# Ten value tiles of an odd layer's projection moved into the seven-product pairs

## The chip, the cores and the metric

The kernel runs on one core of one Trainium2 chip. Its time is the device time of one execution in microseconds; a run's figure is compared by the median. The core has a matrix engine (PE, with a queue of weight loads PEld), a vector engine (DVE), an activation engine (ACT), a general engine (POOL), and a sync engine (SP) whose queue issues most DMAs. PE multiplies a 128 x 128 tile of weights that it has loaded with a moving tile of up to 512 columns and accumulates in PSUM. Each engine takes its instructions in one order, fixed when the program is compiled.

## The reference

One step of a two-layer trunk over 512 sample tokens and 128 prompt tokens, model width 2048, all in float32. Layer 0 has windowed attention (A) and a short gated convolution (B), layer 1 has differential attention (C) and dense attention with normed queries and keys (D). What matters here is layer 1:

```python
def odd_mixer(h, w_in, w_out, cqn, ckn, c_lam, c_on, dqn, dkn, lam_init, ctx=None, rope=None):
    cq, ck, cv, cg, dq, dk, dv, dg = split_cols(h @ w_in, ODD_SPLIT)
    ...
        cv_all = jnp.concatenate([ctx[1], cv], axis=2)
        dv_all = jnp.concatenate([ctx[3], v_d], axis=2)
    ...
    o1 = attend(cq[:, 0][:, :, None], ck_all[:, 0], cv_all)[:, :, 0]
    o2 = attend(cq[:, 1][:, :, None], ck_all[:, 1], cv_all)[:, :, 0]
    o_c = rms_norm(o1 - lam.astype(o1.dtype) * o2, c_on) * (1.0 - lam_init)
    y_c = o_c.transpose(0, 2, 1, 3).reshape(b, t, C_W) * jax.nn.silu(cg)
    y_d = merge_heads(attend(q_d, dk_all, dv_all)) * jax.nn.silu(dg)
    return jnp.concatenate([y_c, y_d], axis=-1) @ w_out, new
```

Each layer also makes a shift, a scale and a gate from `silu(cond) @ ada_w + ada_b` (the conditioning). The prompt tokens' new keys and values are outputs too. C has 4 heads, each with two maps of 128-wide queries and keys and one 256-wide value; D has 8 query heads and 2 heads of keys and values, 128 wide. So the projection of layer 1 has 8 + 8 + 8 + 8 tiles of 128 columns for cq, ck, cv, cg, and 8 + 2 + 2 + 8 for dq, dk, dv, dg: 52 tiles, ten of them values.

## The kernel before

All 640 tokens lie along the moving side as two halves of 320 (`HALF`). A projection tile is one block of 128 output columns; its sum runs over 16 row blocks of 128 (`KT`). Float32 accuracy comes from splitting both operands into a high and a low part (`split`, lines 240 to 242: ACT writes the high part, DVE the rest) and adding three products, high x high, high x low and low x high (lines 276 to 278). The weights of a tile come in four "quarters" of four row blocks, 256 KB each; SP reads them up to five quarters ahead (`RAW_AHEAD`) and they are split three ahead (`SPLIT_AHEAD`).

There are two ways to compute a tile. `run_tiles` (line 312) takes them singly. `run_pairs` (line 435) takes two tiles at once: weights and tokens are cut into 2 x 2 blocks, and seven products of sums of blocks stand for eight (a scheme of Winograd's and Strassen's kind, named Q1, Q2, N5, P6, P7, P4, Q3). DVE forms the sums of weight blocks and adds the results; the sums of the token blocks are formed once in advance (`forms`, tiles T0 to T7).

Layer 1 runs in these stages. `project` (line 1114) computes "front" tiles: 14 of the 16 gate tiles, first three as leading tiles while the rows h are made, then three singly, then eight in four pairs. A gate's result goes to the scratch `gdram` in DRAM (`gate_out`, `front_begin`, `front_done`). Then `run_tiles` computes 38 single tiles: q, k, v in the order of the attention, and last the two gates 4 and 5 (`very_late_gate`). Then `project_out(1, ...)` multiplies by the output weights: three leading tiles, during which the 16 row blocks of y are read back from `ydram` and split (`y1_maker`), three single tiles, and five pairs.

The work between the quarters is a set of generators. After each quarter `slot` (line 301) advances `prep` (a finished tile's own work, such as `k_gen` or `v_gen`), then `attn` (attention: one step each time the pace has summed up to 1), then the conditioning `fill` (`ada_on_dve`: a step reads 128 KB and makes two multiply-adds of 128 x 256 on DVE, line 213; each of its four blocks of 33 steps is tied to the weights split at its start). Attention takes 12 steps for a pair of D's heads (`pair_gen`) and 13 for a head of C (`diff_gen`), a step being roughly the scores and softmax of one block of 128 queries and the value products of the block before. In the stage of 38 tiles the attention takes one step a quarter, 1.5 in the last two tiles; the conditioning takes one step a quarter from the 17th quarter on. The order that a program states is a priority: the framework's planner may put later instructions first where an earlier one isn't ready, within the buffers that there are.

A value tile's `v_gen` copies the projection from PSUM to a buffer (`stage`), transposes it to rows (five transposes), splits it into `vh` and `vl` beside the cached values (`ctx_v`), writes the prompt's rows out, and starts the attention that needs it. Before a head's keys or values are overwritten, `drain(attn)` takes all steps that are left.

Of the kernel before, what the change touches and what calls it, by code (L numbers as in the profile page):

```python
# [48 lines left out]
FILL1 = 1.0  # L49
FILL1_FROM = 16  # L50
# [3 lines left out]
def trunk_kernel(ctx: ExitStack, tc: tile.TileContext, I: dict, O: dict):  # L54
# [523 lines left out]
    def k_gen(ap, pp, tag, src, gain, new_out):  # L578
        raw = ap.tile([P, 2, P], F32, tag="ctxk", name="ctxk", bufs=1)
        nc.sync.dma_start(raw, src.rearrange("(c p) d -> p c d", p=P))  # L580
        x = stage(ap, pp)
        yield
# [39 lines left out]
        split(hi[:, CTX + NS:CTX + NT], lo[:, CTX + NS:CTX + NT], t)  # L622

# [48 lines left out]
    def v_gen(ap, pp, src, new_out, w=P, j=0, then=None):  # L672
        x = stage(ap, pp)
        yield
        if j == 0:
            drain(attn)
            st["v"] = tuple(ap.tile([P, 7, w], F32R, tag=t, name=t) for t in ("vh", "vl"))
            ctx_v(ap, src, *st["v"], w)
        hi, lo = st["v"]
        cols = slice(j * P, (j + 1) * P)  # L680
        t = to_rows(cols_of(x), True)
        split(hi[:, 2:6, cols], lo[:, 2:6, cols], t.rearrange("p (b f) -> p b f", b=4))
# [3 lines left out]
        split(hi[:, 6, cols], lo[:, 6, cols], vp)  # L686
        nc.gpsimd.dma_start(new_out, vp)
        if then:
            attn.append(then())
# [141 lines left out]
    xdram, hdram, gdram = ([dram.tile([P, NT], F32, name=f"{n}{k}") for k in range(KT)] for n in ("xd", "hd", "gd"))  # L831
# [95 lines left out]
    def k_job(tag, src, gain, new_out):  # L927
        return lambda pp: k_gen(pools["cur"], pp, tag, src, gains[gain], new_out)
# [185 lines left out]
    def project(w, cols, n0, maker, job, begin, part, done, tail, **kw):  # L1114

        go_on = run_tiles([(cols[n], job(n)) for n in range(3)], w, maker, **{"order": (0, 2, 1, 3), **kw})


        quarters = [(cols[n], qd) for n in range(3, n0) for qd in range(4)]
# [10 lines left out]
        for n in range(3, n0):  # L1130
            pp, t = new_pp((n - 3) % 2), 4 * (n - 3)
# [262 lines left out]
    N_FRONT = 6  # L1394

# [8 lines left out]

    def front_job(n):
# [6 lines left out]
    def front_begin(p):  # L1412
        for t in range(2):
            outs[t] = gate_out(N_FRONT + 2 * p + t)
# [15 lines left out]
    project(I["od_w_in"][0], [(OD["cg"] + i * P) if i < 8 else OD["dg"] + (i - 8) * P for i in FRONT], N_FRONT, h1_maker,  # L1430
# [31 lines left out]
    for n in range(4):  # L1462
# [4 lines left out]
        if n % 2 == 0:  # L1467
            jobs.append((OD["dk"] + kv * P, k_job(f"k{kv}", I["cache_d_k"][0, 0, kv], "d_k_norm", O["new_d_k"][0, 0, kv])))
            jobs.append((OD["dv"] + kv * P, v_job(I["cache_d_v"][0, 0, kv], O["new_d_v"][0, 0, kv], P, 0, then)))
    for h in range(4):  # L1470
        for m in range(2):
            jobs.append((OD["cq"] + (m * 4 + h) * P, q_job(f"q{m}", "c_q_norm")))
        for m in range(2):
            jobs.append((OD["ck"] + (m * 4 + h) * P,
                         k_job(f"k{m}", I["cache_c_k"][0, 0, m, h], "c_k_norm", O["new_c_k"][0, 0, m, h])))
        for j in range(2):
            jobs.append((OD["cv"] + h * 256 + j * P,
                         v_job(I["cache_c_v"][0, 0, h], O["new_c_v"][0, 0, h][:, j * P:(j + 1) * P], 256, j,
                               diff_then(h) if j else None)))
# [7 lines left out]
    drain(attn)  # L1487


    def y1_maker(k):  # L1490
# [9 lines left out]
        else:  # L1500
            t = pools["cur"].tile([P, 768], F32, tag="P", name="yin", bufs=P_BUFS)[:, 0:NT]
# [34 lines left out]
    project_out(1, y1_maker, rows_out, rows_last, lambda name: None, order=(0, 2, 3, 1))  # L1536
# [49 lines left out]
```

## Time and profile before

| | |
|---|---|
| median of 3 runs | 2317.88 us (2314.68 to 2318.4) |
| profiled execution | 2318.59 us, its span 2316.8 us |
| PE busy | 2272.1 us, 98% of the span |
| DVE busy | 1635.5 us, 71% |
| ACT busy | 969.7 us, 42% |
| mean granted clock of PE | 0.997 |

The span runs from the first to the last instruction of one execution. A row of groups gives line, engine, operation, tiles and shapes, count, busy time, mean ns of one, and the idle time before them with what ended it. A row of windows gives a stretch (us from the span's start), its length, the busy time of PE, PEld, DVE, ACT and POOL with their instructions, the granted clock as a share of full speed, the DMA engines' busy share, and GB/s. By the writes to `gdram` the front tiles of layer 1 end at about 1317 us; the stage of 38 tiles and its attention reach to about 2095 us, and the reads of y for the output projection begin at 2085.5 us.

### The profile page before, as it was taken

To read this page: it belongs to the slowest core of one execution; us is meant where nothing else is said; L and a number is where in the kernel's file an instruction comes from. 1 tells how busy PE (TensorE), PEld (TensorE's weight loads), DVE (VectorE), ACT (ScalarE), POOL (GpSimd) and SP (SyncE) were. 2 spreads that over 40 slices of the span, in tenths; PEclk is the share of its full clock that TensorE was granted. 3 is DMA by queue.
4 is the path that set the end of the run, shared out by engine and by line. 5 is a ranking of instruction groups with operands and counts; after the bars stand their busy time and mean duration, and the time that the engine had idled before them with its cause. 6 is when DMAs were issued, how large, how long until landed. Compare 5 with 4: busy or idle time off the path is not lost.

```text
span 2316.8 us, 41604 instructions
## 1 busy us (share of the span) xinstructions
PE 2272.1 (98%) x15892; PEld 2197.3 (95%) x15892; DVE 1635.5 (71%) x3308; ACT 969.7 (42%) x2007; POOL 175.6 (8%) x243
## 2 busy tenths in 40 slices
PE   7999999999999999999999999999999999999999
PEld 5699999999999999999999999999999999999999
DVE  4559886786866663988887658659657658557576
ACT  4335442433422222544644445555453444434343
POOL 2111000000000000000100000000001010100101
PEclk9999999999999999999999999999999999999999
DMA  9874545445455543844773433224315233318532
GB/s 364 330 260 130 154 124 163 144 122 165 121 180 160 152 139 114 283 140 127 242 223 107 135 102 97 63 81 131 97 52 153 66 92 113 92 60 281 176 119 70
DMA packets 388456, 342.94 MB, mean 148 GB/s; under 512 B 19298, under 2 KB 327024, under 8 KB 387744
## 3 DMA queue, kind: packets, MB, share of 16 engines
q1 hardware_dynamic: 376000, 294.35, 41.9%
q0 software_dynamic: 11536, 43.77, 5.0%
q8 instruction: 125, 2.05, 0.4%
q10 hardware_dynamic: 720, 2.16, 0.3%
q14 instruction: 75, 0.61, 0.1%
HBM read 301.93 MB, written 38.28 MB: 147 GB/s over the span
## 4 chain that ended last, share of the span: by engine, by line
PE 86%; DVE 4%; ACT 3%; DMA 3%; issue 2%; POOL 1%; SPq 0%; ACTq 0%; POOLq 0%; DVEq 0%
PE pa L276 9%; PE pb L277 9%; PE pb L276 9%; PE pa L277 9%; PE pb L278 9%; PE pa L278 9%; PE pq L535 5%; PE pq L537 5%; PE pq L536 5%; PE T L715 2%; PE T L178 1%; PE S L727 1%; PE S L729 1%; PE S L728 1%; DMA yin<-yd 1%
## 5 line engine op out<-in xcount | busy, mean ns | idle before, releaser
L241 ACT ACTIVATE wh<-raw 128x512 fp32r<-128x512 f32 (+1 forms) x466 | 288.4, 619 | 723.8 <-PE pb L277 615.4
L276 PE MATMUL pa<-h,wh 128*128 128x320 f32 x1632 | 519.2, 319 | 4.8 <-ACT h L908 2.5
L242 DVE TENSOR_TENSOR wl<-raw,wh 128x512 fp32r<-128x512 f32 (+1 forms) x466 | 313.8, 674 | 296.3 <-ACT wh L241 260.9
L277 PE MATMUL pa<-h,wh 128*128 128x320 f32 x1632 | 508.3, 312 | 2.8 <-DVE h L242 2.7
L278 PE MATMUL pa<-h,wl 128*128 128x320 f32 x1632 | 506.9, 311 | 0.0
L278 PE MATMUL pb<-h,wl 128*128 128x320 f32 x1632 | 505.5, 310 | 0.0
L276 PE MATMUL pb<-h,wh 128*128 128x320 f32 x1632 | 505.2, 310 | 0.0
L277 PE MATMUL pb<-h,wh 128*128 128x320 f32 x1632 | 505.0, 309 | 0.0
L213 DVE SCALAR_TENSOR_TENSOR acc<-adaw,sT,acc 128x512 f32<-128x512 f32 (+1 forms) x600 | 358.3, 636 | 14.0 <-DMA adaw<-in_ada_w 13.7
L276 PEld LDWEIGHTS pa<-h,wh 128*128 128x128 f32 x1632 | 307.9, 189 | 18.2 <-issue 9.3
L277 PEld LDWEIGHTS pa<-h,wh 128*128 128x128 f32 x1632 | 308.4, 189 | 7.3 <-DVE h L242 4.5
L278 PEld LDWEIGHTS pa<-h,wl 128*128 128x128 f32 x1632 | 307.9, 189 | 3.3 <-issue 3.3
L278 PEld LDWEIGHTS pb<-h,wl 128*128 128x128 f32 x1632 | 306.6, 188 | 2.1 <-issue 2.1
L276 PEld LDWEIGHTS pb<-h,wh 128*128 128x128 f32 x1632 | 306.7, 188 | 0.0
L277 PEld LDWEIGHTS pb<-h,wh 128*128 128x128 f32 x1632 | 306.5, 188 | 0.1
L535 PE MATMUL pq<-h,wh 128*128 128x320 f32 x480 | 149.7, 312 | 0.4 <-DVE xr L1099 0.2
L536 PE MATMUL pq<-h,wh 128*128 128x320 f32 x480 | 148.4, 309 | 0.0
L537 PE MATMUL pq<-h,wl 128*128 128x320 f32 x480 | 148.0, 309 | 0.0
L701 ACT ACTIVATE p<-S,nm,rq 128x768 f32<-128x768 f32 (+3 forms) x120 | 101.2, 843 | 101.4 <-DVE nm L696 67.1
L535 PE MATMUL pq<-T,wh 128*128 128x320 f32 x360 | 111.2, 309 | 0.0
L536 PE MATMUL pq<-T,wh 128*128 128x320 f32 x360 | 111.2, 309 | 0.0
L537 PE MATMUL pq<-T,wl 128*128 128x320 f32 x360 | 111.2, 309 | 0.0
(326 smaller groups left out, 3699.8 us busy)
## 6 DMA issues: line engine op xcount, KB each, us to landing
adaw<-in_ada_w SPq DMA_DIRECT2D x192, 256.0 KB, 3.0
raw<-in_ev_w_in SPq DMA_DIRECT2D x184, 256.0 KB, 3.0
raw<-in_od_w_in SPq DMA_DIRECT2D x184, 256.0 KB, 2.9
ada<-in_ada_w SPq DMA_DIRECT2D x14, 2048.0 KB, 10.5
adaw<-in_ada_w SPq DMA_DIRECT2D x128, 128.0 KB, 2.2
yd<-y POOLq DMA_DIRECT2D x32, 320.0 KB, 3.0
yin<-yd SPq DMA_DIRECT2D x32, 320.0 KB, 4.4
w<-yd SPq DMA_DIRECT2D x32, 320.0 KB, 4.1
```

Source lines behind the costliest of these rows:

```text
L178: PE.matmul(acc[32 * g:32 * g + 32, 0:wd], sT[:, kt, :], w[:, kt % m, :], start=(i < 4), stop=(i >= KT - 4), tile_position=(0, 32 * g))
L213: V.scalar_tensor_tensor(out=a, in0=w, scalar=sT[:, kt, c:c + 1], in1=a, op0=ALU.mult, op1=ALU.add)
L241: A.activation(hi, x, AF.Copy)
L242: V.tensor_sub(lo, x, hi)
L276: PE.matmul(ps, wh[:, i, :], hi[:, sl], start=(j == js[0] if alone else (pos == 0 and j == 0)), stop=False)
L277: PE.matmul(ps, wh[:, i, :], lo[:, sl], start=False, stop=False)
L278: PE.matmul(ps, wl[:, i, :], hi[:, sl], start=False, stop=(j == js[1] - 1 if alone else (pos == 3 and j == 3)))
L535: PE.matmul(ps, wh[:, j, :], hi, start=(h == 0 and j == 0), stop=False)
L536: PE.matmul(ps, wh[:, j, :], lo, start=False, stop=False)
L537: PE.matmul(ps, wl[:, j, :], hi, start=False, stop=(h == 1 and j == 3))
L701: A.activation(p[:, 0:n], s, AF.Exp, scale=rsc, bias=nm, accum_out=l)
L715: PE.transpose(t[:, i * P:(i + 1) * P], p, ident)
```

## The change

The ten value tiles leave the stage of single tiles and are appended to the front tiles, where they form five more pairs. A finished value tile is copied to `sq` or `acc`, transposed to rows in the front stage (`value_rows`), written to a new scratch `vdram` and, for the prompt, to the output. `k_gen` reads the rows back (`v_in`, one tile for D, two for C), splits them together with the cached values after its keys, and starts the attention (`then`). The stage of single tiles has 28 tiles, 112 quarters. In it the attention takes 1.35 steps a quarter in the first 13 tiles, 1.1 in the next 13, and 1.5 in the last two as before; the conditioning takes 1.33 steps from the first quarter. The attention is no longer drained behind the last tile; the output projection has two leading tiles (the third used PSUM that scores use), and its first reads of y go to other buffers (`rp`, `stg` in place of `P`).

```diff
-FILL1 = 1.0
-FILL1_FROM = 16
+FILL1 = 1.33
+FILL1_FROM = 0
...
-    def k_gen(ap, pp, tag, src, gain, new_out):
+    def k_gen(ap, pp, tag, src, gain, new_out, vals=None, then=None):
+
+        vx = []
+
+        def v_in(j):
+            vx.append(ap.tile([P, 5, P], F32, tag="stg", name="vx", bufs=2))
+            nc.sync.dma_start(vx[j].rearrange("p b f -> p (b f)"), vals[1][j])
+
         raw = ap.tile([P, 2, P], F32, tag="ctxk", name="ctxk", bufs=1)
         nc.sync.dma_start(raw, src.rearrange("(c p) d -> p c d", p=P))
         x = stage(ap, pp)
+        if vals:
+            v_in(0)
         yield
...
+        if vals and len(vals[1]) == 2:
+            v_in(1)
...
+        if vals:
+            yield
+            w = P * len(vals[1])
+            hi, lo = st["v"] = tuple(ap.tile([P, 7, w], F32R, tag=t, name=t) for t in ("vh", "vl"))
+            ctx_v(ap, vals[0], hi, lo, w)
+            for j in range(len(vx)):
+                cols = slice(j * P, (j + 1) * P)
+                split(hi[:, 2:7, cols], lo[:, 2:7, cols], vx[j])
+        if then:
+            attn.append(then())
...
-    def project(w, cols, n0, maker, job, begin, part, done, tail, **kw):
+    def project(w, cols, n0, maker, job, begin, part, done, tail, n_lead=3, **kw):
...
+    VALUES = [(OD["dv"] + i * P, O["new_d_v"][0, 0, i]) for i in range(2)]
+    VALUES += [(OD["cv"] + i * P, O["new_c_v"][0, 0, i // 2][:, i % 2 * P:(i % 2 + 1) * P]) for i in range(8)]
...
+    def value_rows(n, t):
+        yield
+        r = pools["cur"].tile([P, 5, P], F32, tag="xr", name="vr", bufs=3)
+        A.copy(r[:, 0:4, :], to_rows(cols_of(st[t]), True).rearrange("p (b f) -> p b f", b=4))
+        A.copy(r[:, 4, :], to_rows(cols_of(st[t]), False))
+        nc.gpsimd.dma_start(vdram[n], r.rearrange("p b f -> p (b f)"))
+        nc.gpsimd.dma_start(VALUES[n][1], r[:, 4, :])
+
+    def value_out(n):
+        def put(t, sl, src):
+            A.copy(st[t][:, sl], src)
+            if (n, "v") in half_done:
+                prep.append(value_rows(n, t))
+            half_done.add((n, "v"))
+        return put
+
...
     def front_begin(p):
         for t in range(2):
-            outs[t] = gate_out(N_FRONT + 2 * p + t)
+            n = N_FRONT + 2 * p + t
+            outs[t] = gate_out(n) if n < len(FRONT) else value_out(n - len(FRONT))
...
-    brisk = {len(jobs), len(jobs) + 1}
+    brisk = {len(jobs): 1.5, len(jobs) + 1: 1.5}
+    brisk.update((i, 1.35 if i < 13 else 1.1) for i in range(len(jobs)))
...
     run_tiles(jobs, I["od_w_in"][0], None, fill1, FILL1, fill_from=FILL1_FROM,
-              steps=lambda i: 1.5 if i in brisk else 1.0)
+              steps=lambda i: brisk.get(i, 1.0))
     drain(prep)
-    drain(attn)
...
-            t = pools["cur"].tile([P, 768], F32, tag="P", name="yin", bufs=P_BUFS)[:, 0:NT]
+            tag, n = (("rp", 3), ("stg", 2))[k % 2]
+            t = pools["cur"].tile([P, NT], F32, tag=tag, name="yin", bufs=n)
...
-    project_out(1, y1_maker, rows_out, rows_last, lambda name: None, order=(0, 2, 3, 1))
+    project_out(1, y1_maker, rows_out, rows_last, lambda name: None, n_lead=2, order=(0, 2, 3, 1))
```

More of the change, by code (lines that the diff above doesn't have):

```diff
@@ L670, in ctx_v, with v_gen @@
         split(hi[:, 0:2, :], lo[:, 0:2, :], raw)
-    def v_gen(ap, pp, src, new_out, w=P, j=0, then=None):
+    def v_gen(ap, pp, src, new_out, then=None):
         x = stage(ap, pp)
         yield
-        if j == 0:
-            drain(attn)
[L677 to L680, printed above, removed]
+        drain(attn)
+        hi, lo = st["v"] = tuple(ap.tile([P, 7, P], F32R, tag=t, name=t) for t in ("vh", "vl"))
+        ctx_v(ap, src, hi, lo, P)
         t = to_rows(cols_of(x), True)
-        split(hi[:, 2:6, cols], lo[:, 2:6, cols], t.rearrange("p (b f) -> p b f", b=4))
+        split(hi[:, 2:6, :], lo[:, 2:6, :], t.rearrange("p (b f) -> p b f", b=4))
         t = to_rows(cols_of(x), False)
@@ L685, in v_gen @@
         V.tensor_copy(vp, t)
-        split(hi[:, 6, cols], lo[:, 6, cols], vp)
+        split(hi[:, 6, :], lo[:, 6, :], vp)
         nc.gpsimd.dma_start(new_out, vp)
@@ L830, in trunk_kernel @@
     x0dram = [dram.tile([P, 4 * NT + 1], F32, name=f"x0d{g}") for g in range(4)]
-    xdram, hdram, gdram = ([dram.tile([P, NT], F32, name=f"{n}{k}") for k in range(KT)] for n in ("xd", "hd", "gd"))
+    xdram, hdram, gdram, vdram = ([dram.tile([P, NT], F32, name=f"{n}{k}") for k in range(KT)]
+                                  for n in ("xd", "hd", "gd", "vd"))
     y = [None] * KT
@@ L924, in even_start, with k_job @@
         open_pool("even")
-    def k_job(tag, src, gain, new_out):
-        return lambda pp: k_gen(pools["cur"], pp, tag, src, gains[gain], new_out)
+    def k_job(tag, src, gain, new_out, *a):
+        return lambda pp: k_gen(pools["cur"], pp, tag, src, gains[gain], new_out, *a)
     def v_job(src, new_out, *a):
@@ L1112, in form_of @@
         return lambda j: (T[j][:, 0, i * HALF:(i + 1) * HALF], T[j][:, 1, i * HALF:(i + 1) * HALF])
-    def project(w, cols, n0, maker, job, begin, part, done, tail, **kw):
-        go_on = run_tiles([(cols[n], job(n)) for n in range(3)], w, maker, **{"order": (0, 2, 1, 3), **kw})
-        quarters = [(cols[n], qd) for n in range(3, n0) for qd in range(4)]
+    def project(w, cols, n0, maker, job, begin, part, done, tail, n_lead=3, **kw):
+        go_on = run_tiles([(cols[n], job(n)) for n in range(n_lead)], w, maker, **{"order": (0, 2, 1, 3), **kw})
+        quarters = [(cols[n], qd) for n in range(n_lead, n0) for qd in range(4)]
         raws, parts = [], []
@@ L1129, in project @@
         go_on()
-        for n in range(3, n0):
-            pp, t = new_pp((n - 3) % 2), 4 * (n - 3)
+        for n in range(n_lead, n0):
+            pp, t = new_pp((n - n_lead) % 2), 4 * (n - n_lead)
             for hv in ([HV] if n < n0 - 1 else [HV[1:], HV[:1]]):
@@ L1484, in trunk_kernel @@
     run_tiles(jobs, I["od_w_in"][0], None, fill1, FILL1, fill_from=FILL1_FROM,
-              steps=lambda i: 1.5 if i in brisk else 1.0)
+              steps=lambda i: brisk.get(i, 1.0))
     drain(prep)
-    drain(attn)
     def y1_maker(k):
```

14 lines of the change are left out of this document (6 added, 8 removed).

## The prediction

> **What bounds the kernel now.** I read the page's busy shares first, then the costliest groups of instructions for their counts.
>
> ```profile
> span 2316.8 us, 41604 instructions
> PE 2272.1 (98%) x15892; PEld 2197.3 (95%) x15892; DVE 1635.5 (71%) x3308; ACT 969.7 (42%) x2007; POOL 175.6 (8%) x243
> ...
> L276 PE MATMUL pa<-h,wh 128*128 128x320 f32 x1632 | 519.2, 319 | 4.8 <-ACT h L908 2.5 <-ACT h L241 2.3
> L535 PE MATMUL pq<-h,wh 128*128 128x320 f32 x480 | 149.7, 312 | 0.4 <-DVE xr L1099 0.2
> L535 PE MATMUL pq<-T,wh 128*128 128x320 f32 x360 | 111.2, 309 | 0.0
> ```
>
> PE is bound nearly everywhere. The matmuls overlap, so 319 ns is not their price; that is the distance of two starts, from the timeline of PE, here with 57 such distances between its two rows:
>
> ```profile
> 1319.74 0.31 PE L277 MATMUL pa<-h,wh 128*128 128x320 f32 x1
> ...
> 1328.10 0.31 PE L277 MATMUL pb<-h,wh 128*128 128x320 f32 x1
> ...
> 2039.62 0.71 PE L564 MATMUL T<-ident,stg 128*128 128x128 f32 x5
> ```
>
> 8.36/57 = 0.1467 us. A single tile has 16 row blocks x 2 halves x 3 = 96 matmuls, 14.08 us; a quarter, 3.52 us. A pair has 7 products x 8 x 3 = 168, and indeed (480 + 360) x 3 = 2520 is 15 pairs of 168. Transposes start (0.71 - 0.27)/4 = 0.11 us apart.
>
> Next the windows, for what the stages have to spare. In order: five stretches of pairs (their sum), a stretch of layer 0 with attention, then four of layer 1's projection and two of its heads in mixer C (columns: length, PE, PEld, DVE, ACT, POOL busy, granted clock, DMA share, GB/s).
>
> ```profile
> sum 130.00, PE 130.00 PEld 129.80 DVE 96.95 ACT 59.92 POOL 5.94; mean PE 26.00 PEld 25.96 DVE 19.39 ACT 11.98 POOL 1.19
> ...
> 300.00:325.00 25.00, 25.00 (x190) 24.54 (x187) 24.73 (x59) 11.04 (x28) 0.00 (x0) 1.00 0.40 116
> ...
> 1320.00:1345.00 25.00, 24.91 (x169) 23.82 (x168) 8.52 (x18) 10.35 (x22) 1.66 (x1) 1.00 0.59 181
> 1395.00:1420.00 25.00, 24.70 (x181) 23.98 (x180) 24.25 (x56) 14.07 (x28) 1.46 (x1) 1.00 0.35 103
> 1770.00:1795.00 25.00, 22.89 (x150) 22.60 (x150) 18.64 (x44) 8.19 (x24) 1.88 (x2) 0.93 0.57 168
> 2045.00:2070.00 25.00, 24.41 (x169) 22.89 (x168) 18.32 (x41) 11.03 (x25) 1.63 (x3) 1.00 0.18 58
> ...
> sum 775.00, PE 762.59 PEld 740.32 DVE 520.49 ACT 367.00 POOL 68.77; mean PE 24.60 PEld 23.88 DVE 16.79 ACT 11.84 POOL 2.22
> ...
> 1689.95:1809.22 119.27, 115.73 (x804) 112.41 (x802) 85.68 (x203) 52.52 (x126) 11.45 (x15) 0.99 0.36 107
> 1924.88:2040.08 115.20, 112.99 (x793) 110.44 (x792) 71.07 (x162) 53.46 (x130) 12.71 (x15) 1.00 0.31 92
> ```
>
> Pairs run without a gap at 75% DVE. Layer 1's projection (the sum of 31 stretches, 1320 to 2095) leaves PE idle 12.4 us in 775. Even a DVE at 24.7 of 25 us can leave PE full (300 to 325).
>
> **The change, part by part.**
>
> *Ten tiles become five pairs.* PE loses 10 x 96 = 960 matmuls and gains 5 x 168 = 840: 120 fewer, at 0.1467 us **-17.6 us**. 40 quarters (140.8 us) leave the projection stage, 123.2 us join the gates. All lie on PE's queue, on the path. The 50 transposes (5 a tile) move from one stage to the other: 5.5 us there, 5.5 us here, 0.
>
> *What the pairs bring to other engines.* 14 weight splits a pair against 8 for two tiles, so 30 more, plus the operand sums.
>
> ```profile
> L242 DVE TENSOR_TENSOR wl<-raw,wh 128x512 fp32r<-128x512 f32 x442 | 304.0, 688 | 284.2 <-ACT wh L241 249.0 <-PE T L564 25.2 <-DMA raw<-in_ev_w_in 7.0
> L242 DVE TENSOR_TENSOR h<-yin,h 128x640 fp32r<-128x640 f32 x32 | 25.8, 819 | 10.6 <-ACT h L241 10.5
> gd<-g POOLq DMA_DIRECT2D x14, 320.0 KB, 3.2
> ```
>
> The gate pairs already have all that, and 6.6 us of each 26 free on DVE; value pairs need no gate product. Hidden behind PE: 0 (uncovered, 30 x 0.688 = 20.6 us). Row copies take ACT's place of the tanh; ACT has 14 us of 26 free. Each tile issues two writes from POOL (320 KB as the gates do, and 64 KB of output), POOL busy 6 of 130 us: 0.
>
> *The value rows come back in the K tile.* One or two 320 KB reads from SP and a 640 wide split each (0.819 us DVE, as for yin) replace the transposes' splits and copy: even. The second read waits in SP's queue for the staging buffer; behind it stand weight reads (five quarters ahead of use, two ahead of the split) and conditioning reads. The next tile's ACT copies wait for the split of that buffer; behind them on ACT stand weight splits, three quarters (10.6 us) ahead. 0 taken; uncovered 0.82 x 10 = 8 us, and below 0 nothing, since PE's work is the same.
>
> *The same attention over 112 quarters instead of 152.* Two heads of D take 12 steps, a head of C 13: 100 in all. Before, one step a quarter; now 1.35 through D, 1.1 in C. The stage shrinks to 775 - 141 = 634 us; its DVE work to 520.5 - 40 x 0.688 = 493 us, 78% (from 67%). The two last tiles run at 1.5 steps already (2045 to 2070): PE is idle 0.59 us in 25, against the stage's mean 12.4/31 = 0.40. So denser attention costs some 0.2 us per 25, over 634 us **+5; I take +2.5**, since C is only at 1.1. The low end is 0, as no step gets more room. What can go further is a gap such as this one, in waits of PE and windows:
>
> ```profile
> PE T L564 <- DVE m L609: 2.1, 1, 2.1
> ...
> 1782.00:1784.00 2.00, 0.79 (x6) 0.55 (x5) 2.00 (x5) 0.90 (x2) 0.59 (x1) 1.00 0.20 47
> 1784.00:1786.00 2.00, 1.09 (x5) 1.10 (x6) 2.00 (x6) 0.00 (x0) 0.00 (x0) 0.75 0.31 96
> 1786.00:1788.00 2.00, 2.00 (x9) 1.96 (x9) 1.57 (x4) 0.60 (x1) 0.00 (x0) 0.50 0.77 230
> 1788.00:1790.00 2.00, 2.00 (x14) 2.00 (x13) 1.60 (x5) 0.70 (x2) 0.00 (x0) 0.89 0.41 118
> ```
>
> A K tile's chain on DVE, mixed with a burst of conditioning, left PE without split weights for 2.1 us, and the granted clock then fell: 2 x (0.25 + 0.50 + 0.11) = 1.7 us more, 3.8 a gap. The Trainium skill ("TensorE: Matmul & The Clock Gate", HAM oscillation) puts the throttle at idle gaps of over about 3.4 us; by it a gap of 2.1 us costs just that. The trace disagrees (0.50 granted after 2.1 us), and the row decides.
>
> *Conditioning at 1.33 from the first quarter.* Its four blocks of 33 steps begin now in quarters 17, 50, 83, 116 and run in bursts (DVE 24.25 of 25 at 1395). Then they begin in 1, 26, 51, 76: the first falls where DVE is idle (8.52 of 25 at 1320), the third again on K tiles, and all 132 steps end by quarter 99. Between -1 and +3.8 (one more gap); 0 taken, the work is the same.
>
> *Output projection with two leading tiles; no drain before it.* The matmuls are the same. The last head's attention starts in the third quarter of the last-but-one tile; six quarters x 1.5 do 9 of its 13 steps, so four spill under the first y reads and cover them, at most (115.2 - 24 x 3.52)/13 = 2.4 us each. But PE now uses up a row block of y in 12 matmuls (1.76 us), not 18 (2.64). Windows before, and two of ACT's waits:
>
> ```profile
> 2100.00:2110.00 10.00, 10.00 (x70) 10.00 (x69) 5.05 (x8) 3.75 (x6) 0.00 (x0) 1.00 0.88 280
> 2110.00:2120.00 10.00, 10.00 (x70) 10.00 (x69) 8.50 (x15) 4.26 (x6) 0.00 (x0) 1.00 0.92 319
> 2120.00:2130.00 10.00, 8.04 (x51) 7.17 (x50) 9.03 (x16) 4.61 (x8) 0.00 (x0) 1.00 0.94 288
> ...
> 2106.34 0.74 ACT L241 ACTIVATE h<-yin 128x640 fp32r<-128x640 f32 x1 [2.95 <-DMA yin<-yd]
> ...
> 2123.97 0.74 ACT L241 ACTIVATE h<-yin 128x640 fp32r<-128x640 f32 x1 [2.66 <-DMA yin<-yd]
> ```
>
> DMA is at 0.88 to 0.94 for these 30 us and PE idles 2.0. With a third of PE's work gone from here (10 us, done later), the bytes, 8.9 MB, fall only by the third tile's two or three weight reads (256 KB, 0.9 us each): PE could wait 10 - 2.5 = 7.5 us more. The spilled steps and the unneeded drain (0.59 us at 2045) work against that: -1 to +7.5, **I take +1.5**, nearer the low end, as 9 us of steps now lie under the first eight reads.
>
> **Sum:** -17.6 + 2.5 + 0 + 1.5 = **-13.6**. The profiled execution took 2318.6 (span 2316.8 and 1.8 around it), 0.7 above the median: 2305.0 for it, **2304.3** for the median.
>
> **Rivals.**
> *A, the y reads take half.* The lead waits the full 7.5: -17.6 + 2.5 + 7.5 = -7.6, **2310**. For: DMA above 0.88. Against: reads of the first blocks can start before the last tile ends.
> *B, slower: the K tiles.* A quarter without attention is 3.52 us of PE against a K tile's chain on DVE, now with value splits in the same four quarters and conditioning at 1.33. If the gap of 2.1 + 1.7 us comes at K tiles, five (19 us) cancel the gain; at all eight of C, 30.4 - 17.6 = +12.8, **2331**. For: it happened at 1784. Against: three further bursts made none. By the skill's rule, without the slow clock, eight gaps would be 16.8, and the time 2317.
> *C, no change: dense attention.* Windows of the 56 quarters that hold D's attention, for all and for the conditioning's line alone:
>
> ```profile
> 1380.00:1689.95 309.95, 307.02 (x2183) 298.56 (x2182) 225.64 (x507) 157.53 (x336) 23.21 (x25) 1.00 0.32 95
> ...
> 1380.00:1689.95 309.95, 50.70 (x116) 1.00 0.32 95
> ```
>
> Twelve of them go (three value tiles): PE 310 - 42 = 268 us. DVE, 174.9 without conditioning, less 12 x 0.688, plus 44 x 1.33 steps of 50.7/58 = 0.87 us, is 218 us: 81% on the mean, more where steps are double. Were 1.7 us lost in each 25, somewhat under the stretch at 1770, the 17.6 would be gone: **2318**. Against: 300 to 325 and 1395 to 1420.
>
> **How the numbers follow.** Forecast (losses up to 7, or gains from the drain: 2297 to 2308) 0.60; A 0.17; C 0.09; B 0.14. A change within 0.2% (4.6 us) cannot be told from none. Faster: forecast and A, 0.77; same 0.09; slower 0.14. The range, 2297 to 2318, leaves out B and a little of each end; its low end is -17.6 with the two gains of 1 and a further 1 of median. The forecast's own is 2297 to 2308.
>
> **What would show it.** Group rows: pq h 640 and T 480, pa 1488 (one leading tile more leaves the third bank pair, Sp from 128 to 96). Pairs full on PE, windows at 26.00 of 26.00. The projection stage near 634 us with idle PE of 10 to 15; above 30 the forecast is wrong (B or C; in B the clock dips below 0.9). In the output projection's lead, PE idle of 2 to 5 us: above 9 is A. If the pairs show gaps on DVE, the first step is wrong.

## The result, and the profile after

The changed kernel takes 2332.72 us (median of 4 runs, 2327.24 to 2333.71) against 2317.41 us before on the same chip: ratio 1.0062, 95% interval 1.0048 to 1.0077. It is 15.3 us slower, where 13.6 us faster was forecast. The profiled execution took 2333.41 us, its span is 2331.6.

The page of the changed kernel: span, busy times, and the groups that count the pairs (columns as before).

```profile
span 2331.6 us, 41517 instructions
PE 2259.4 (97%) x15772; PEld 2178.4 (93%) x15772; DVE 1689.7 (72%) x3378; ACT 995.0 (43%) x2052; POOL 184.9 (8%) x253
...
L276 PE MATMUL pa<-h,wh 128*128 128x320 f32 x1488 | 473.6, 319 | 18.6 <-ACT h L241 16.2
...
L535 PE MATMUL pq<-h,wh 128*128 128x320 f32 x640 | 199.8, 312 | 0.7 <-ACT wh L241 0.7
...
L535 PE MATMUL pq<-T,wh 128*128 128x320 f32 x480 | 148.4, 309 | 0.0
```

PE has the 120 matmuls fewer (15892 to 15772) and is busy 12.7 us less, yet the span is 14.8 longer. The one new item stands in the first group: PE's wait for the split of h rose from 2.3 to 16.2 us.

Where the time went is read from three marks in each kernel: the last matmul of layer 1's pairs, the last gate tile's tanh (the end of the stage of single tiles), and the first matmul of the output's pairs with low weights (L537). Rows of lines, with min/median/max ns and the first and last start; first the kernel before, then the changed one.

```profile
L537 PE MATMUL pq<-h,wl x286: 307/309/311, 999.9 to 1314.6; 128*128 128x320 f32 x143
L1452 ACT ACTIVATE gt_t<-pb x1: 432/432/432, 2091.1 to 2091.1; 128x320 f32<-128x320 f32 x1
L537 PE MATMUL pq<-h,wl x160: 305/309/312, 2182.6 to 2311.5; 128*128 128x320 f32 x160
```

```profile
L537 PE MATMUL pq<-h,wl x451: 303/309/312, 1000.1 to 1443.1; 128*128 128x320 f32 x151
...
L1491 ACT ACTIVATE gt_t<-pb x2: 421/422/422, 2052.8 to 2082.4; 128x320 f32<-128x320 f32 x2
...
L537 PE MATMUL pq<-h,wl x160: 307/309/313, 2197.7 to 2326.5; 128*128 128x320 f32 x160
```

| part | before | after | difference | the work moved |
|---|---|---|---|---|
| up to the pairs' end | 1314.6 | 1443.1 | +128.5 | +123.2 + 5.5 = +128.7 |
| stage of single tiles | 776.5 | 639.3 | -137.2 | -140.8 - 5.5 - some 6.5 = -152.8 |
| lead of the output projection | 91.5 | 115.3 | +23.8 | some +6.5 |
| from the output's first pair on | 134.2 | 133.9 | -0.3 | 0 |

The pairs are as forecast, though the agreement to 0.2 us is luck: in the profiles of the later runs that share these pairs they end between 1439.5 and 1446.4. In the two middle parts 137.2 - 23.8 = 113.4 us were saved where 146.3 us of work left: 32.9 us are lost there. How much of it is the stage's and how much the lead's is read from windows of both, first before and then after (columns: length, PE, PEld, DVE, ACT, POOL busy, granted clock, DMA share, GB/s):

```profile
1320.00:2091.10 771.10, 758.70 (x5320) 736.45 (x5318) 516.81 (x1176) 363.98 (x824) 68.22 (x80) 1.00 0.32 95
...
2091.10:2182.60 91.50, 89.30 (x608) 88.08 (x609) 63.95 (x116) 39.22 (x69) 9.23 (x14) 1.00 0.79 251
```

```profile
1450.00:2082.40 632.40, 608.42 (x4248) 581.89 (x4247) 475.58 (x1092) 322.01 (x740) 65.51 (x68) 1.00 0.33 102
...
2082.40:2197.70 115.30, 98.95 (x666) 95.97 (x665) 72.61 (x139) 45.04 (x83) 10.96 (x16) 0.97 0.64 204
```

The lead has 58 matmuls more (666 against 608), nearly all of them value products, scores and transposes of attention that ran in the stage before. At 0.11 to 0.12 us each, that is 6 to 7 us of work that crossed the border; the table counts them. So about 16 us are lost in the stage and 17 in the lead; with marks that shift by up to 3 us from one profile to the next, the two are about equal, and only their sum is firm. Of the stage's loss 11.6 us are idle time of PE (12.4 before, 24.0 after); the slow clock adds nothing there, since either kernel has one stretch of 25 us at 0.93 (1770 before, shown in the prediction; 1500 after, shown below). Where in PE's busy time the other 4 lie isn't shown. Of the lead's loss 14.2 are idle time (2.2 before, 16.4 after) and some 1.5 slow clock.

Which waits grew, from PE's waits between 1450 and 2095 us (total us, times, longest), before and after:

```profile
PE T L1368 <- DVE on L1362: 4.7, 9, 0.8
PE T L564 <- DVE m L609: 2.4, 3, 2.1
```

```profile
PE T L1387 <- DVE on L1381: 8.6, 8, 1.8
PE T L564 <- DVE m L620: 4.6, 4, 2.8
PE S L745 <- ACT p L719: 3.5, 7, 0.6
PE T L564 <- DVE k1l L242: 2.4, 3, 1.1
```

All are links of PE with the attention and the K tiles, none with a weight split: the stage has lost slack in many short waits, not in one.

The lead first. PE's waits there, in the changed kernel from 2095 to 2200 us:

```profile
PE pa L276 <- ACT h L241: 11.2, 3, 8.3
PE T L564 <- DVE xr L1118: 3.3, 2, 2.0
```

Before, the waits of this part came to 2.1 us, none over 0.9. So one gap makes over half of it; the others follow it, two more for y's rows and two for the residual that a finished tile is added to (xr).

The gap in detail. Timelines of SP's queue, of POOL and of PE in the changed kernel (start, duration, engine, line, operation; in brackets the idle time before and what ended it), and its windows:

```profile
2098.62 9.58 SPq L254 DMA_DIRECT2D raw<-in_od_w_out  x4
2108.29 1.48 SPq L1123 DMA_DIRECT2D yin<-yd  x3
```

```profile
2107.50 1.11 POOL L857 DMA_DIRECT2D yd<-y  x2 [2.47 <-DVE y L1392]
```

```profile
2115.09 0.64 PE L276 MATMUL pa<-h,wh 128*128 128x320 f32 x1 [8.35 <-ACT h L241]
```

```profile
2100.00:2110.00 10.00, 6.74 (x48) 6.50 (x46) 3.54 (x9) 2.05 (x5) 1.66 (x3) 1.00 0.38 108
...
2110.00:2113.00 3.00, 0.00 (x0) 0.00 (x0) 0.00 (x0) 0.00 (x0) 0.00 (x0) 0.72 1.00 350
2113.00:2116.00 3.00, 0.92 (x3) 0.83 (x4) 0.94 (x2) 1.58 (x3) 0.00 (x0) 0.50 0.93 366
2116.00:2119.00 3.00, 3.00 (x15) 2.98 (x15) 2.93 (x6) 0.94 (x2) 0.00 (x0) 0.64 0.73 234
```

PE stands for 8.35 us, then runs its first matmuls at a granted clock of 0.50 to 0.64. It waits for the read of y's block 12, issued at 2108.29 (the row blocks come in the order 0 to 3, 8 to 11, 12 to 15, 4 to 7). Two things let go of that read within a microsecond of each other: four weight reads ahead of it in SP's queue, which themselves wait for VectorE's splits (9.58 us), and the last head's attention, whose y is written at 2107.50. Blocks 12 to 15 go to buffers of the pool `fin`, which takes the place of the attention's pool `odd`; it opens once all attention is done. Before, the same sequence ran 7 to 9 us earlier, with three leading tiles to cover it:

```profile
2098.99 0.54 POOL L838 DMA_DIRECT2D yd<-y  x1 [0.50 <-issue]
...
2101.45 1.78 SPq L1104 DMA_DIRECT2D yin<-yd  x3
```

The late start is not the whole wait. From the issue to ACT's first split of these rows (2114.30) another 6.0 us pass, with the DMA engines at 1.00 from 2110 to 2113: reads that were held up together also move together, right behind y's last write.

### The profile page after: what moved, and what is told of

Its sections match the earlier page's. It is cut to its first block, busy times and chain, and to the rows that moved or that the text cites. A ratio compares the mean times of both kernels' runs of the same rounds, so it can differ in the third digit from the quotient of the medians.

```text
span 2331.6 us, 41517 instructions
## 1 busy us (share of the span) xinstructions
PE 2259.4 (97%) x15772; PEld 2178.4 (93%) x15772; DVE 1689.7 (72%) x3378; ACT 995.0 (43%) x2052; POOL 184.9 (8%) x253
## 3 DMA queue, kind: packets, MB, share of 16 engines
q10 hardware_dynamic: 720, 2.16, 0.3%
## 4 chain that ended last, share of the span: by engine, by line
PE 81%; DVE 7%; DMA 5%; ACT 3%; issue 2%; POOL 1%; SPq 0%; ACTq 0%; POOLq 0%; DVEq 0%
PE pa L276 8%; PE pb L277 8%; PE pb L276 8%; PE pa L277 8%; PE pb L278 8%; PE pa L278 8%; PE pq L535 7%; PE pq L537 7%; PE pq L536 7%; PE T L733 2%; DMA adaw<-in_ada_w 2%; DVE acc L213 2%; PE T L178 1%; PE S L745 1%; DMA yin<-yd 1%
## 5 line engine op out<-in xcount | busy, mean ns | idle before, releaser
L276 PE MATMUL pa<-h,wh 128*128 128x320 f32 x1488 | 473.6, 319 | 18.6 <-ACT h L241 16.2
L277 PE MATMUL pa<-h,wh 128*128 128x320 f32 x1488 | 464.1, 312 | 0.6 <-DVE h L242 0.4
L278 PE MATMUL pa<-h,wl 128*128 128x320 f32 x1488 | 463.1, 311 | 0.0
L278 PE MATMUL pb<-h,wl 128*128 128x320 f32 x1488 | 462.1, 311 | 0.0
L277 PE MATMUL pb<-h,wh 128*128 128x320 f32 x1488 | 461.5, 310 | 0.0
L276 PE MATMUL pb<-h,wh 128*128 128x320 f32 x1488 | 461.2, 310 | 0.0
L276 PEld LDWEIGHTS pa<-h,wh 128*128 128x128 f32 x1488 | 280.6, 189 | 32.9 <-ACT h L241 18.2
L277 PEld LDWEIGHTS pa<-h,wh 128*128 128x128 f32 x1488 | 281.2, 189 | 4.5 <-DVE h L242 2.0
L276 PEld LDWEIGHTS pb<-h,wh 128*128 128x128 f32 x1488 | 280.3, 188 | 0.0
L277 PEld LDWEIGHTS pb<-h,wh 128*128 128x128 f32 x1488 | 280.1, 188 | 0.1
L535 PE MATMUL pq<-h,wh 128*128 128x320 f32 x640 | 199.8, 312 | 0.7 <-ACT wh L241 0.7
L536 PE MATMUL pq<-h,wh 128*128 128x320 f32 x640 | 197.8, 309 | 0.0
L537 PE MATMUL pq<-h,wl 128*128 128x320 f32 x640 | 197.7, 309 | 0.0
L537 PE MATMUL pq<-T,wl 128*128 128x320 f32 x480 | 148.4, 309 | 0.0
L536 PE MATMUL pq<-T,wh 128*128 128x320 f32 x480 | 148.4, 309 | 0.0
L535 PE MATMUL pq<-T,wh 128*128 128x320 f32 x480 | 148.4, 309 | 0.0
```

Source lines behind the costliest of these rows:

```text
L276: PE.matmul(ps, wh[:, i, :], hi[:, sl], start=(j == js[0] if alone else (pos == 0 and j == 0)), stop=False)
L277: PE.matmul(ps, wh[:, i, :], lo[:, sl], start=False, stop=False)
L278: PE.matmul(ps, wl[:, i, :], hi[:, sl], start=False, stop=(j == js[1] - 1 if alone else (pos == 3 and j == 3)))
L535: PE.matmul(ps, wh[:, j, :], hi, start=(h == 0 and j == 0), stop=False)
L536: PE.matmul(ps, wh[:, j, :], lo, start=False, stop=False)
L537: PE.matmul(ps, wl[:, j, :], hi, start=False, stop=(h == 1 and j == 3))
```

## The experiments

Each ran beside the kernel before, whose medians were 2317.4 to 2318.8 us. What a kernel gains against the changed one is the difference of their ratios to before (1.0062 for the changed kernel), times 2318 us.

**The lead: is it the new entry into the output projection?**

`e1_old_entry` undoes the entry alone; `e2_entry_alone` puts it alone into the kernel before.

```diff
# e1, on the changed kernel (e2 is the reverse, on the kernel before)
     drain(prep)
+    drain(attn)
...
-            tag, n = (("rp", 3), ("stg", 2))[k % 2]
-            t = pools["cur"].tile([P, NT], F32, tag=tag, name="yin", bufs=n)
+            t = pools["cur"].tile([P, 768], F32, tag="P", name="yin", bufs=P_BUFS)[:, 0:NT]
...
-    project_out(..., n_lead=2, order=(0, 2, 3, 1))
+    project_out(..., order=(0, 2, 3, 1))
```

> The changed kernel with the entry into the output projection as it was: three leading tiles, the attention drained behind the last tile, y's first reads in the buffers P. The trace of the changed kernel shows two losses beside the gain of 17.6 us: some 17.6 us between the last projection tile and the first output pair, and some 15 us in the projection stage. Theory (y's reads for block 12 on stand in SP's queue behind weight reads, and two tiles use up y faster than it comes): the lead gets back most of its loss, but the four steps that are drained without cover cost some 8 to 10 us: 2322 to 2326. Rival (the lead's loss comes from the spilled attention steps, however many tiles lead): the steps are late in any case, 2331 or more.

> The kernel before with the new entry alone: two leading tiles, no drain, y's first reads in rp and stg; value tiles and rates as before, so only about one attention step is left for the lead. Theory (two tiles use up y faster than SP's queue brings it): 8 to 15 us slower than before, 2325 to 2333. Rival (the spilled steps are the cause): within 3 us of before, 2315 to 2320.

Measured: e1 2324.83, ratio 1.0027 [1.0017, 1.0038], 8 us better than the changed kernel; e2 2325.82, 1.0035 [1.0023, 1.0047], 8 us worse than before. The entry costs 8 us in either direction, with all of its parts at once. What is left of the loss in e1 is mostly the stage's, and the drain itself: there PE has nothing beside the last attention steps. Windows of e1:

```profile
2090.00:2100.00 10.00, 6.19 (x33) 5.58 (x34) 5.25 (x16) 3.21 (x9) 0.94 (x2) 0.76 0.31 98
2100.00:2110.00 10.00, 9.89 (x62) 9.62 (x62) 7.71 (x14) 6.55 (x12) 1.66 (x3) 0.90 0.74 230
2110.00:2120.00 10.00, 10.00 (x71) 10.00 (x70) 6.42 (x11) 3.75 (x6) 0.00 (x0) 1.00 0.94 305
```

The wait for y is gone (10.00 of 10.00 at 2110); in its place the drain idles PE 3.8 us and lowers the clock.

**The lead: buffers, queue, or the DMA engines?** `e6_fin_late` opens the pool `fin` at block 4, the first of the last quarter, so that blocks 12 to 15 are read into the old pool's buffers as well; `e9_fin_last` reads all 16 blocks there and opens `fin` at the very end.

```diff
# e6_fin_late
-        if k == 12:
+        if k == 4:
...
-        if k % 8 >= 4:
+        if 4 <= k < 8:
             late_yin(k)
```

```diff
# e9_fin_last
-        if k % 8 >= 4:
-            late_yin(k)
-        else:
-            tag, n = (("rp", 3), ("stg", 2))[k % 2]
...
+        tag, n = (("rp", 3), ("stg", 2))[k % 2]
...
+        if k == 7:
             close("odd")
             open_pool("fin")
```

> The changed kernel, with the buffers of the output stage opened four row blocks later (at block 4, the last quarter, in place of block 12): y's blocks 12 to 15 are read into the buffers of blocks 0 to 11 and need not wait for the pool, and the planner can place their reads ahead of the weight reads. Theory (the gap of 8.35 us and the slow clock behind it come from the place of these reads in SP's queue): 8 to 12 us faster than the changed kernel, 2320 to 2325. Rival (the DMA engines can't bring y faster, whatever the order): within 3 us of the changed kernel, 2330 to 2336.

> The changed kernel with the output stage's buffers opened only behind the last row block of y: all sixteen reads go to rp and stg. With the opening at block 4 it took 2322.8 us and PE still waited where the last four reads stood behind four weight reads. Theory (the place in SP's queue sets the gap): another 2 to 6 us less, 2317 to 2321. Rival (the DMA engines' rate sets it by now): 2321 to 2325; the residual reads, which come later, could also cost 1 to 3 us.

Measured: e6 2322.79, 1.0025 [1.0015, 1.0036], 9 us better than the changed kernel. e9 2325.95, 1.0038 [1.0025, 1.0051], which misses the theory's 2317 to 2321: with `fin` open only at the end, the residual is read later still, and PE's wait for it is 4.7 us against 3.0 in e6. The row of PE's waits in e9's lead (total, times, longest):

```profile
PE T L564 <- DVE xr L1118: 4.7, 1, 4.7
```

So the late reads of blocks 12 to 15 are a cause of some 9 us, and there is a best place for the opening. But e6 moves these reads past the pool's opening and past the weight reads alike. Three kernels separate the two: `e5_y_on_pool` issues the late reads on POOL's queue, `e13_drain` ends the attention ahead of the leading tiles and leaves the queue, `e14_drain_pool` does both.

```diff
# e5_y_on_pool (and e14), in late_yin; "pool_y" is set where fin is opened
-        nc.sync.dma_start(t, ydram[k])
+        (nc.gpsimd if st.get("pool_y") else nc.sync).dma_start(t, ydram[k])
```

```diff
# e13_drain (and e14)
     drain(prep)
+    drain(attn)
```

> The changed kernel with the reads of y's row blocks 12 to 15 issued on POOL's DMA queue in place of SP's; all else as it is. Theory (in SP's queue these reads stand behind four weight reads that wait 9.58 us for VectorE): they start earlier, PE's 8.35 us of idle time in the lead falls below 4 us, and the time is 2322 to 2328. Rival (the DMA engines are full there, so the reads land no earlier from another queue): the idle time stays at 7 to 9 us, 2330 to 2335.

> The changed kernel with the attention drained ahead of the two leading tiles again; reads and buffers as in the changed kernel. Theory (both must go: buffers that open after the last attention at 2107.2 us, and SP's queue behind weight reads to 2108.2 us): the idle time of 8.35 us in the lead shrinks by under 3 us, the drain costs PE 2 to 5 us, and the time is 2330 to 2337. Rival (the buffers alone hold the reads): the idle time falls below 3 us, 2324 to 2329.

> As e13_drain, and the y reads of blocks 12 to 15 and 4 to 7 on POOL's queue. Theory (both causes gone): the idle time in the lead falls below 3 us, 2321 to 2328. Rival (the DMA engines or the reads' own time bind): it stays at 6 to 9 us, 2330 to 2337.

Measured: e5 2327.44, 1.0034 [1.0020, 1.0048]; e13 2331.43, 1.0060 [1.0045, 1.0075]; e14 2327.28, 1.0045 [1.0029, 1.0062]. POOL's queue and PE in e5:

```profile
2110.34 1.11 POOL L857 DMA_DIRECT2D yd<-y  x2 [2.48 <-DVE y L1392]
2111.45 1.66 POOL L1123 DMA_DIRECT2D yin<-yd  x3
```

```profile
2117.87 0.64 PE L276 MATMUL pa<-h,wh 128*128 128x320 f32 x1 [8.29 <-ACT h L241]
```

In e5 the reads no longer stand behind weight reads, and start no earlier (25.7 us after the last gate's tanh, 25.9 in the changed kernel): they follow the attention's last write, and the idle time stays at 8.29. The write and the reads are now on one queue, so e5 can't tell whether the pool's opening holds the reads or POOL's own order does. The theory of the queue alone fell here as to the first wait, though e5's median is 5 to 6 us lower. Its trace shows what became shorter: PE's other waits for y's rows fall from 2.9 us to 0.5, and the wait for the residual from 3.3 to 0.3. The profiled execution was still the slowest of its five (2332.47), with a longer stage (642.7 us). SP's queue and PE in e13:

```profile
2108.36 0.37 SPq L254 DMA_DIRECT2D raw<-in_od_w_out  x1
2108.82 1.41 SPq L1123 DMA_DIRECT2D yin<-yd  x3
```

```profile
2113.00 0.63 PE L276 MATMUL pa<-h,wh 128*128 128x320 f32 x1 [5.92 <-ACT h L241]
```

In e13 the attention's y is done at 2104 and written from 2104.62, but now the weight reads hold SP until 2108.73. So the reads start no earlier than in the changed kernel, and yet the idle time falls to 5.92: the three reads land in 3.7 us (median), against 6.3. What differs is that y's last writes began 4.2 us ahead of them, not 0.8, so the load of the DMA engines is probably a part of the wait as well. The drain takes the gain back. With both gone (e14: reads of blocks 12 to 14 issued from 2103.34) the first gap is down to 4.21, but a second one follows:

```profile
2108.92 0.41 PE L276 MATMUL pa<-h,wh 128*128 128x320 f32 x1 [4.21 <-ACT h L241]
...
2114.18 0.64 PE L277 MATMUL pa<-h,wh 128*128 128x320 f32 x1 [4.56 <-DVE h L242]
```

```profile
2112.90 0.49 DVE L1104 TENSOR_TENSOR tables<-w 128x320 f32<-128x320 f32 x1 [6.95 <-DMA w<-yd]
2113.31 0.82 DVE L242 TENSOR_TENSOR h<-yin,h 128x640 fp32r<-128x640 f32 x1
```

VectorE stands 6.95 us before an operation of `forms`, which waits for its own read of y, and the split that PE needs is queued behind it. So e14's theory (under 3 us) fell as well, though its time lies in the range that went with it. The lead has three bounds close together, the end of the attention (through the pool's opening, and on POOL's queue through its order), SP's order, and VectorE's order behind the other reads of y; taking one or two away brings the next. e6 gains more than all these, though its late reads start no sooner (2108.73): with blocks 12 to 15 early, PE has four more row blocks to use up before the late ones, 48 matmuls or 7 us.

**The stage: conditioning or density?** `e3_after_no_cond` leaves out the four late conditioning blocks of the changed kernel, `e4_before_no_cond` the same of the kernel before, so that both compute with a constant gate in layer 1. `e7_spread` keeps the conditioning and ties every fourth step to the weights split at that time, which breaks its bursts.

```diff
# e3, e4
-    fill1 = ada_on_dve(ada_rest[N_FILL0:], ("acc0", "acc1", "adaw", "adaw", "adaw", "adaw"), 2,
-                       lambda: mark[-1])
+    fill1 = iter(())
+    V.memset(hgt[1], 0.25)
```

```diff
# e7, in ada_on_dve
+                late = tie()
+                if late is not None and i % 4 == 3:
+                    V.tensor_copy(w[:, 0:1], late)
```

> The changed kernel without the conditioning of layer 1's gates (the four late blocks, 132 steps on DVE and their reads, are left out and a constant stands for their result). To be read against the next run, the kernel before without the same. Theory (DVE's load by conditioning lengthens the chains that PE waits for in the projection stage): the 14 us lost there shrink to under 5, so that this kernel is within 6 us of the next (the loss in the output projection's lead, some 18 us, stays and about cancels the gain of 17.6). Rival (too little projection work stands between two attention steps, whatever DVE does beside): the loss stays, and this kernel is 12 to 17 us slower than the next.

> The kernel before without the conditioning of layer 1's gates, as in the run above. It prices the same work where PE had more projection to cover it: PE's waits for attention and K tiles in the projection stage come to some 10 us, so both theories expect 2 to 8 us less than before, 2309 to 2315.

> The changed kernel, with every fourth step of layer 1's late conditioning tied to the weights that are split at its place in the order (a copy of one column into the buffer before it is read, 32 copies of some 0.15 us), so that a block of 33 steps can no longer run as a burst. Theory (bursts on DVE that meet a K tile's chain make the gaps in the projection stage): 5 to 10 us faster than the changed kernel, 2323 to 2328. Rival (the denser attention itself makes them): within 3 us, 2330 to 2336.

Measured: e3 2315.59, 0.9986 [0.9977, 0.9996]; e4 2307.73, 0.9959 [0.9944, 0.9974]; e7 2335.52, 1.0076 [1.0061, 1.0091]. Without conditioning the change costs 7.9 us in place of 15.3. That lies between the two expectations, so each has a part. (e4 itself came out lower than expected: leaving the conditioning out also takes some 6 us of PE's own work away, the same in both kernels.) Windows of the stage, e4 and then e3:

```profile
1320.00:2081.80 761.80, 752.25 (x5279) 733.03 (x5277) 423.17 (x900) 362.92 (x820) 67.86 (x80) 1.00 0.25 74
```

```profile
1450.00:2065.20 615.20, 601.32 (x4201) 578.43 (x4201) 383.21 (x816) 321.50 (x736) 63.78 (x68) 1.00 0.26 77
```

PE's idle time is 9.6 and 13.9 us: 4.3 more with the change, where it was 11.6 with conditioning. So some 7 us of the stage's loss are the conditioning on top of the attention's greater density (7.4 by the medians, 7.3 by the idle time). The density by itself makes the rest, 4.3 us as idle time and some 8 or 9 by the marks, where the stage's whole loss is 16. e7 says that it is not the bursts as such: broken up, the stage is hardly shorter (637.9 us between its marks against 639.3). That theory fell.

`e8_sparse` lowers the attention's pace, `e10_later_fill` starts the conditioning later.

```diff
# e8_sparse
-    brisk.update((i, 1.35 if i < 13 else 1.1) for i in range(len(jobs)))
+    brisk.update((i, 1.2 if i < 13 else 1.0) for i in range(len(jobs)))
```

```diff
# e10_later_fill
-FILL1 = 1.33
-FILL1_FROM = 0
+FILL1 = 1.4
+FILL1_FROM = 16
```

> The changed kernel with 1.2 attention steps a quarter in the first 13 tiles and 1.0 in the next 13, in place of 1.35 and 1.1. Some steps are then left over at the K tiles and taken there in one go, about one for each of the seven. Theory (the density of steps makes the waits): fewer slots with two steps, but the leftover steps come together; 0 to 5 us faster than the changed kernel, 2328 to 2333. Rival (conditioning or the K tiles make them): the left-over steps only add waits, 2333 to 2340.

> The changed kernel with layer 1's conditioning at 1.4 steps a quarter from the 17th quarter on, in place of 1.33 from the first. Theory (the first block's burst collides with mixer D's first K tile, where PE idles 2.84 us at 1502 and the granted clock falls to 0.93 over 25 us): that gap is gone, and the time falls by 2 to 4 us, 2328.5 to 2331. Rival (the block collides somewhere else, or the K tile's own chain makes the gap): 2332 to 2335, with a gap of 2 to 3 us at a K tile as before.

Measured: e8 2330.13, 1.0056 [1.0039, 1.0072]; e10 2324.57, 1.0030 [1.0019, 1.0041]. In e8 the stage ends 6.5 us earlier (2075.9) with PE idle for 20.5 us, but 3.6 of these come from before the stage, where the two kernels are the same. The gain is 1.4 us by the ratios and 2.6 by the medians, which their intervals don't tell from none. e10 answers a row of the changed kernel, where the first conditioning block meets D's first K tile (timeline of PE, and windows there):

```profile
1502.32 0.66 PE L564 MATMUL T<-ident,m 128*128 128x128 f32 x4 [2.84 <-DVE m L620]
```

```profile
1500.00:1502.00 2.00, 0.00 (x0) 0.00 (x0) 2.00 (x5) 0.06 (x1) 0.28 (x1) 1.00 0.08 33
1502.00:1504.00 2.00, 1.39 (x9) 1.12 (x9) 2.00 (x6) 0.60 (x1) 0.00 (x0) 0.94 0.57 168
1504.00:1506.00 2.00, 1.76 (x7) 1.77 (x8) 1.58 (x4) 0.28 (x1) 0.00 (x0) 0.50 0.11 33
1506.00:1508.00 2.00, 2.00 (x12) 2.00 (x11) 0.00 (x0) 0.85 (x2) 0.00 (x0) 0.70 0.43 127
```

The same stretch, changed kernel first, then e10:

```profile
1500.00:1525.00 25.00, 22.15 (x143) 21.10 (x144) 18.14 (x38) 11.98 (x25) 1.98 (x2) 0.93 0.21 61
```

```profile
1500.00:1525.00 25.00, 24.86 (x173) 23.78 (x172) 21.48 (x49) 13.45 (x27) 2.25 (x2) 1.00 0.31 93
```

This gap is gone, as expected, but its like came up at a K tile of C in e10, with a granted clock of 0.50 behind it (1956 to 1958), which is the rival's sign:

```profile
1955.05 0.81 PE L564 MATMUL T<-ident,m 128*128 128x128 f32 x4 [2.16 <-DVE m L620]
```

PE's waits for m come to 4.4 us, against 4.6. The gain is larger than expected all the same: 7 us by the ratios. In the profiles, 5.2 us apart, the stage is 5.7 us shorter between its marks, the lead 2.8 shorter, and the part before both 3.3 longer. So a later start helps, but not by the gap that it was meant for; which waits it saves, and why the lead gains too, is open.

**Do the cures add?** `e11_both` joins e6, e8's pace, e10 and the reads of e5; `e15_both_drain` adds e13's drain to it; `e12_old_lead` joins e1, e8 and e10. Their edits are those shown.

> Four edits on the changed kernel at once: the buffers of the output stage opened after y's row block 4 in place of 12 (alone: -10 us), attention at 1.2 and 1.0 steps a quarter (alone: -2.6 us in the time, -6.5 us in the projection stage), conditioning at 1.4 steps from the 17th quarter, and the y reads of blocks 4 to 7 on POOL's queue. Theory (two separate losses, in the projection stage and in the lead of the output projection, whose cures add): 2312 to 2319, level with the kernel before or just under it. Rival (what the stage gains is lost again where the attention left over runs beside the lead): 2320 to 2326.

> The changed kernel with the old entry into the output projection (three leading tiles, attention drained ahead of it, y read into the old buffers; alone: -8 us), attention at 1.2 and 1.0 steps a quarter and conditioning at 1.4 steps from the 17th quarter. Theory (the cures add): 2317 to 2322. Rival (the sparser attention leaves more steps to the drain, in which PE has nothing else to do): 2323 to 2328.

> As e11_both (2315.34), with the attention drained ahead of the two leading tiles. Theory (there the reads of blocks 12 to 15 are early anyway, so the drain only costs): 2316 to 2320. Rival (the last four reads still wait for the attention's end at 2102): 2311 to 2315.

Measured: e11 2315.34, 0.9991 [0.9981, 1.0000]; e12 2318.48, 1.0001 [0.9992, 1.0011]; e15 2313.90, 0.9980 [0.9970, 0.9991]. The cures come to 16 us in e11 and 14 in e12, where the single ones (e6 or e1, e8, e10) add up to 17 each, the reads on POOL's queue not counted. In e15 the drain, which was worth nothing alone, seems to bring 1 to 3 us more (the intervals overlap): the last four reads still followed the attention's end in e11. Windows of e15:

```profile
2100.00:2110.00 10.00, 7.66 (x53) 7.39 (x51) 2.49 (x4) 4.05 (x6) 1.74 (x4) 1.00 1.00 331
2110.00:2120.00 10.00, 9.82 (x55) 9.57 (x56) 8.99 (x18) 3.29 (x5) 0.54 (x1) 0.83 0.90 297
```

e15 beats the kernel before by 0.2%, about 4.6 us: a quarter of the 17.6 us that the pairs save. Its lead (last gate at 2075.9, first output pair at 2178.5) is still 102.6 us against 91.5 before, of which 6 to 7 are the attention that crossed the border, and the stage still idles 19.5 us. The kernel before was not tuned in the same ways.

## Why the prediction was wrong, by its steps

- **Ten tiles become five pairs, -17.6: right.** 120 matmuls went, the pairs' end moved by 128.5 us (128.7 worked out, within the 3 us by which profiles differ), and the counts came out as named: pq h 640, T 480, pa 1488. The pairs kept PE full with the value tiles' work beside them, so the 0 for other engines held.
- **Output projection with two leading tiles, +1.5 with bounds -1 and +7.5: this step failed.** It measured about 17, with PE idle for 16.4 us in the lead, where over 9 was named as the sign of A. It priced the bytes that the DMA engines must move while PE runs through y, and took the four spilled attention steps as cover. It never asked when the second eight reads may start. They need a pool that opens after the last attention, so the very steps counted as cover delayed them; and they stand behind weight reads in SP's queue, which the change part should have named. The bound of 7.5 was no bound, since it counts bytes alone: a read that starts late costs its delay even where the engines have room (DMA was at 0.38 from 2100 to 2110), and then its time to land on top (6.0 us). Rival A had the right place; its mechanism is at most a part, and its size was too small. Its sentence "reads of the first blocks can start before the last tile ends" was true of eight blocks and not of the other eight.
- **The same attention over 112 quarters, +2.5: the term was mis-sized.** The stage lost about 16 us, with 24.0 us of idle PE where 10 to 15 was named. The 0.2 us per 25 came from two tiles late in the stage, where conditioning had long run out. e3 and e4 put the density alone at 4.3 us of idle time and some 8 or 9 by the marks, so the +5 at which the bound stood was at best just enough; the other 7 are density and conditioning together, which the working had priced apart.
- **Conditioning from the first quarter, 0 with bounds -1 and +3.8: failed.** The first block was said to fall where DVE is idle. It met D's first K tile at 1502 (2.84 us, then a clock of 0.50), and e10 shows 5 to 7 us for starting later, not all of it at that gap.
- **Rival B gave the time (2331) for mostly another reason.** The waits for a K tile's chain (m) rose only from 2.4 to 4.6 us over the stage; one gap of over 2 us came, not eight. C's doubt about dense attention was right in direction, with 8 to 16 us in place of 17.6. The sum, -17.6 + 16 + 17, is +15.4.

The page "TensorE: Matmul & The Clock Gate" of the Trainium skill (HAM oscillation) has the rule that PE should have no idle gaps of over about 3.4 us. At 1502 the slow clock came after 2.84 us, so this trace too disagrees with that figure; after the 8.35 us in the lead the two agree.

## What to carry to other kernels

When work moves out of a stage whose end feeds a hand-over (reads that wait for a pool to close, for a queue, for a last write), price the hand-over by when its first transfer may start, not by its bytes alone; work that spills into it is cover only if nothing waits for its end. Filler that is free beside a loose schedule isn't free beside a tight one: its price is a property of the sum, so bound it from the tightest stretch with both loads, and look at which tile its first block will meet. And when several bounds lie within a microsecond of each other, taking one away need not shorten the wait; bring the need later, or take them away together.

## What the runs showed of the hardware that was not expected

The granted clock can answer short gaps: 0.50 in the windows after a gap of 2.84 us at 1502, and still 0.70 two microseconds later, so a gap of 2.84 us costs some 1.5 us more (1.76 x 0.50 + 2 x 0.30 of busy time) in slow matmuls. A drain brings such gaps: in e1 there are two, of 2.18 and 2.69 us, and they left the clock at 0.76 and 0.90 over two stretches of 10 us, some 2.5 us more on PE's busy time (6.19 x 0.24 + 9.89 x 0.10). Length alone doesn't decide: a gap of 2.16 us in e10 was followed by 0.50, one of 2.29 us in the changed kernel's lead, which ended at 2126.08, by 1.00. What sets the two apart these runs don't show.

The reads of y's blocks 12 to 14 (320 KB each) took 3.7 to 6.4 us from issue to landing (medians): 5.4 to 6.4 where the last two writes of y began 0.8 to 1.1 us ahead of them (the changed kernel, e5, e14), 5.1 where they began 3.5 us ahead (the kernel before), 3.7 where it was 4.2 us (e13). That the writes are the reason is read from this order, not tested.
